# Shared keys as seven block products per pair of heads, the key gain in the norm, and the second adaLN's chunks at other places

## The chip, the cores and the metric

The kernel runs on one core of a Trainium2 chip. Its engines are TensorE (PE in the profile; PEld is its weight load), VectorE (DVE), ScalarE (ACT), GpSimd (POOL) and SyncE (SP), which issues most DMAs. The metric is the device time of one execution in microseconds. Times below are medians of runs, and where the profile is meant, those of one profiled execution.

## The reference, cut to what matters

One step of a two-layer encoder for 512 prompt tokens and 8 x 16 sample tokens (640 together, D = 2048, 16 heads of 128). Layer 0 is a recurrent layer, layer 1 an attention layer with keys and values that come from layer 0's output `x`:

```python
def ada_mod(c, w, b):
    m = jax.nn.silu(c) @ w + b
    shift, scale, gate = jnp.split(m, 3, axis=-1)
...
def shared_kv(x, g_kv, w_kv):
    k, v = jnp.split(rms_norm(x, g_kv) @ w_kv, 2, axis=-1)
...
def run_group(...):
    for l in range(DEPTH):
        shift, scale, gate = ada_mod(c, w_ada[l], b_ada[l])
        hn = rms_norm(x, g_pre[l]) * (1.0 + scale) + shift
        if l < N_A:
            out, hT, cb = recurrent_mixer(hn, ...)
        else:
            k_new, v_new = shared_kv(x, g_kv, w_kv)
            ...
            out = stick_breaking_mixer(hn, k_all, v_all, w_in_b[j], w_out_b[j])
        x = x + gate * rms_norm(out, g_post[l])
```

All is float32. `w_kv` is 2048 x 4096: keys for 16 heads, then values.

## The kernel before

Products in float32 accuracy are made of three in `fp32r`: each operand is split into a high part (ACT copies it, L87) and a low part (DVE subtracts, L88), and `mm3` (L101 to L103) adds high x high, high x low and low x high in PSUM. Weights pass through this split on the way: DMA into `wr`, `hilo` into `wh` and `wl`, three buffers each.

The stages after the recurrent layer, in order:

- *First output product* (`out_product`, tiles `acc`): the lower half of the rows of `w_out_a`, four chunks of 512 columns, all five token tiles; 16 K tiles in steps of two. At the end of each step of chunks 1 to 3 it advances a generator `fill` once.
- *Second output product*: the upper half, eight chunks (three token tiles x four columns, then two x four).
- *The norm* (`mid`): for each token tile t, residual, row norm, then for each of four column blocks n a scaled tile `nt`, four PE transposes into PSUM (`pst`, two banks), ACT's copy `nh` and DVE's rest `nl`. These, as `hT`, are the moving or stationary operand of all later products. POOL computes the powers of the row norms (`ss`, `sr`, L290) and issues the stores of `x1d`.
- *Shared keys and values* (`shared_kv`): `values(0)`, then `keys(h)` for 16 heads, then `values(1)` to `values(3)` (all tiles `acck`). A column of values is 16 K tiles x 5 token tiles x 3 products of 128x512; a head of keys is 16 K tiles x 2 halves of 320 tokens x 3 products of 128x320. The gain `g_kv` goes into the weights: for v within the split (L1029, L1030), for k by a POOL product over the raw weights (L1037). In `values(3)` `query_norm` turns `hT` in place into the attention layer's input, from the sum of `nh` and `nl`.

adaLN's vectors for layer 1 (and the gate of layer 0) are 16 chunks of 512 columns of `w_ada`. A chunk is four groups; a group (`ada`) loads two raw tiles `wa` (512 KB each), splits each into three bf16 parts (two ACT casts L185, two DVE subtractions L186), and runs 12 matmuls `psa` (L198) of 32 columns at four column places. Groups come from the `fill` generator: layer 0's gate in the first output product, the other 12 chunks (`ada_rest`) in the keys and in `values(1)` to `values(3)`.

The recurrent layer's input product already forms pairs of output blocks by a seven-product scheme (`pair_product`, `pair_weights`, `seven`): for a pair of 128-column blocks and 14 of the 16 K tiles, seven block products stand for eight; the two remaining K tiles are plain. Sums of weight quarters are made by DMAs that add (POOL's queue).

The order on each engine is set when the program is built, by a scheduler that works with estimated durations; on the chip every engine runs its own list strictly in that order, and a wait holds up all that stands behind it.

Of the kernel before, what the change touches and what calls it, by code (L numbers as in the profile page):

```python
# [19 lines left out]
P = 128  # L20
D = 2048
# [27 lines left out]
class Trunk:  # L49
# [32 lines left out]
    def hilo(self, raw, width):  # L82
# [4 lines left out]
        nc.scalar.activation(hi[:, :n], raw, AF.Copy)  # L87
        nc.vector.tensor_tensor(lo[:, :n], raw, hi[:, :n].bitcast(F32), ALU.subtract)  # L88
# [3 lines left out]
    def wraw(self, src, width):  # L92
        n = src.shape[1] * width
        raw = self.wp.tile([P, self.WW], F32, tag="wr", name="wr", bufs=self.RB)
        v = raw[:, :n].rearrange("p (a n) -> p a n", n=width)
        self.nc.sync.dma_start(v, src)
        return v
# [80 lines left out]
    def ada_split(self, src):  # L178

        nc = self.nc  # L180
        raw = self.adap.tile([P, 2, 512], F32, tag="wa", name="wa", bufs=self.abufs[0])
        nc.sync.dma_start(raw, src)
        parts = [self.adap.tile([P, 2, 512], BF16, tag=f"wa{i}", name=f"wa{i}", bufs=self.abufs[1]) for i in range(3)]
# [5 lines left out]
    def ada(self, w):  # L189
# [3 lines left out]
        ps = self.bank("psa")  # L193
        for g in range(4):
            ws = [self.ada_split(w[:, k : k + 2, :]) for k in (4 * g, 4 * g + 2)]
            for i in range(3):
                for j in range(4):
                    nc.tensor.matmul(ps[32 * j : 32 * j + 32, :], self.c3[:, 4 * g + j, :], ws[j // 2][i][:, j % 2, :],  # L198
                                     start=g + i == 0, stop=g == 3 and i == 2)
# [5 lines left out]
    def ada_cols(self, w, dst):  # L205

        for m in self.ada(w):
# [47 lines left out]
    def ada_gate(self, l, c):  # L255

        nc, I = self.nc, self.I
        for m in self.ada(I["w_ada1"][12 * l + c]):
# [14 lines left out]
    def ada_gates(self, l):  # L273
        for c in range(4):
            yield from self.ada_gate(l, c)

    def ada_rest(self):

        for part, dst in ((0, self.sh1), (1, self.gs1)):
            for c in range(4):  # L280
                dsts = [self.ada_dst(1, part, k, dst) for k in range(4 * c, 4 * c + 4)]
                yield from self.ada_cols(self.I["w_ada1"][4 + 4 * part + c], dsts)
        yield from self.ada_gates(1)
# [62 lines left out]
    def start(self, rp):  # L346
# [19 lines left out]
        for k in range(KD):  # L366
# [55 lines left out]
            elif k < 2 * NP:  # L422
                self.combine(rp, slot, even, tmp)
# [10 lines left out]
    def combine(self, rp, slot, even, odd):  # L434
# [3 lines left out]
        t = [rp.tile([P, HALF], F32, tag=f"s{i}", name=f"s{i}", bufs=1) for i in range(4)]  # L438
# [1120 lines left out]
```

## Time and profile before

| | us |
|---|---|
| median of 3 runs | 2882.94 (2881.82 to 2884.23) |
| profiled execution | 2886.43 |
| its span | 2884.3 |
| granted TensorE clock, mean | 0.996 |
| DMA | 546.33 MB, mean 189 GB/s |

The span reaches from the first instruction to the end of the last; the 2.1 us beyond it are the launch. Shares are of the span. A matmul's duration in the profile is a modelled latency; matmuls overlap, so what one costs is the distance from its start to the next one's. "PE busy" counts these overlapped records.

### The profile page before, as it was taken

Reading aid. Unit: us, or ns where it says so; the run is one execution under the profiler, and the core shown is the slowest. Engines: PE = TensorE matmul, PEld = TensorE weight load, DVE = VectorE, ACT = ScalarE, POOL = GpSimd, SP = SyncE. Lnnn points to the kernel's source line nnn. Section 1 sums busy time; section 2 is a strip of 40 time slices with the busy share of each in tenths; the row PEclk is TensorE's granted clock in tenths of the full one; section 3 lists DMA queues with packets and bytes.
Section 4 is the critical chain, followed back from the end, with each engine's and each line's share of the span. In section 5 each row is a group of like instructions: output and inputs, shape, how many; then the busy total and the mean of one; then the engine's idle time right before and its main releaser. Section 6 shows DMA issues by size and latency. Waiting matters only on the chain.

```text
span 2884.3 us, 48196 instructions
## 1 busy us (share of the span) xinstructions
PE 2826.2 (98%) x18784; PEld 2514.8 (87%) x18784; DVE 1965.5 (68%) x2865; ACT 1605.6 (56%) x2464; POOL 415.3 (14%) x604
## 2 busy tenths in 40 slices
PE   6999999999999999999999999999999999998998
PEld 5799999999999987788778999778989889996787
DVE  7678767777777767543678777767766677666235
ACT  5476556655665566443566666753555555555223
POOL 0012211221122100001114221001000001101000
PEclk9999999999999999999999999999999999999999
DMA  9966766676667565654757666654556656567637
GB/s 328 331 146 156 165 160 156 157 165 160 154 158 165 121 243 184 186 181 131 251 188 239 212 215 208 214 173 145 175 177 195 197 184 194 172 209 273 174 110 226
DMA packets 249363, 546.33 MB, mean 189 GB/s; under 512 B 23000, under 2 KB 107096, under 8 KB 247984
## 3 DMA queue, kind: packets, MB, share of 16 engines
q1 hardware_dynamic: 221216, 446.92, 48.5%
q0 software_dynamic: 27920, 96.34, 15.7%
q8 instruction: 147, 2.41, 0.3%
q14 instruction: 80, 0.66, 0.1%
HBM read 501.15 MB, written 42.02 MB: 188 GB/s over the span
## 4 chain that ended last, share of the span: by engine, by line
PE 86%; DVE 3%; DMA 2%; ACT 1%; issue 1%; POOL 0%; SPq 0%; DVEq 0%; POOLq 0%; ACTq 0%
PE acc L101 6%; PE acc L103 6%; PE acc L102 6%; PE psh L101 5%; PE acck L101 5%; PE psh L103 5%; PE psh L102 5%; PE acck L102 5%; PE acck L103 5%; PE pa L101 3%; PE pa L103 3%; PE pa L102 3%; PE pc L103 2%; PE pc L101 2%; PE pc L102 2%; PE psa L198 2%
## 5 line engine op out<-in xcount | busy, mean ns | idle before, releaser
L88 DVE TENSOR_TENSOR wl<-wr,wh 128x1024 fp32r<-128x1024 f32 x216 | 269.7, 1251 | 306.0 <-ACT wh L87 305.6
L87 ACT ACTIVATE wh<-wr 128x1024 fp32r<-128x1024 f32 x216 | 228.1, 1057 | 408.2 <-PE acc L103 257.2
L101 PE MATMUL acc<-wh,yh 128*128 128x512 f32 x960 | 376.8, 393 | 3.1 <-ACT wh L87 3.0
L102 PE MATMUL acc<-wl,yh 128*128 128x512 f32 x960 | 375.3, 391 | 3.5 <-DVE wl L88 3.5
L103 PE MATMUL acc<-wh,yl 128*128 128x512 f32 x960 | 373.9, 390 | 1.3 <-DVE yl L837 1.3
L101 PE MATMUL psh<-nh,wh 128*128 128x320 f32 x1024 | 324.1, 317 | 0.0
L186 DVE TENSOR_TENSOR wa<-wa,wa 128x1024 bf16<-128x1024 f32 (+1 forms) x256 | 306.4, 1233 | 22.0 <-ACT wa L185 20.0
L103 PE MATMUL psh<-nh,wl 128*128 128x320 f32 x1024 | 319.0, 312 | 0.0
L102 PE MATMUL psh<-nl,wh 128*128 128x320 f32 x1024 | 317.6, 310 | 0.0
L185 ACT ACTIVATE wa<-wa 128x1024 bf16<-128x1024 f32 x256 | 263.1, 1052 | 61.6 <-DVE wa L186 42.7
L101 PEld LDWEIGHTS acc<-wh,yh 128*128 128x128 f32 x960 | 180.2, 188 | 50.6 <-issue 8.5
L102 PEld LDWEIGHTS acc<-wl,yh 128*128 128x128 f32 x960 | 180.6, 188 | 42.9 <-DVE wl L88 6.2
L103 PEld LDWEIGHTS acc<-wh,yl 128*128 128x128 f32 x960 | 180.6, 188 | 39.2 <-DVE yl L837 1.7
L101 PEld LDWEIGHTS psh<-nh,wh 128*128 128x128 f32 x1024 | 192.4, 188 | 19.3 <-DVE ql L1183 12.6
L103 PE MATMUL pa<-xs,wl 128*128 128x320 f32 x630 | 194.9, 309 | 0.5 <-DVE wl L88 0.5
L102 PE MATMUL pa<-xs,wh 128*128 128x320 f32 x630 | 194.8, 309 | 0.0
L101 PE MATMUL pa<-xs,wh 128*128 128x320 f32 x630 | 194.8, 309 | 0.0
L103 PEld LDWEIGHTS psh<-nh,wl 128*128 128x128 f32 x1024 | 192.5, 188 | 0.5 <-DVE wl L88 0.2
L102 PEld LDWEIGHTS psh<-nl,wh 128*128 128x128 f32 x1024 | 192.4, 188 | 0.1
L101 PE MATMUL acck<-nh,wh 128*128 128x320 f32 x512 | 161.6, 316 | 0.0
L103 PE MATMUL acck<-nh,wl 128*128 128x320 f32 x512 | 158.3, 309 | 0.0
L102 PE MATMUL acck<-nl,wh 128*128 128x320 f32 x512 | 158.2, 309 | 0.0
(357 smaller groups left out, 7213.6 us busy)
## 6 DMA issues: line engine op xcount, KB each, us to landing
wa<-w_ada_dram SPq DMA_DIRECT2D x192, 512.0 KB, 4.6
wr<-w_out_a_dram SPq DMA_DIRECT2D x96, 512.0 KB, 4.0
sum<-w_in_a_dram POOLq DMA_DIRECT2D x90, 448.0 KB, 5.6
wr<-w_in_b_dram SPq DMA_DIRECT2D x64, 512.0 KB, 5.5
ck<-cache_k_dram SPq DMA_DIRECT2D x64, 512.0 KB, 6.8
cv<-cache_v_dram SPq DMA_DIRECT2D x64, 512.0 KB, 5.4
wr<-w_out_b_dram SPq DMA_DIRECT2D x56, 512.0 KB, 3.8
raw<-w_in_a_dram SPq DMA_DIRECT2D x60, 448.0 KB, 4.2
```

Source lines behind the costliest of these rows:

```text
L87: nc.scalar.activation(hi[:, :n], raw, AF.Copy)
L88: nc.vector.tensor_tensor(lo[:, :n], raw, hi[:, :n].bitcast(F32), ALU.subtract)
L101: mm(out, sh, mh, start=start, stop=False, **kw)
L102: mm(out, sh, ml, start=False, stop=False, **kw)
L103: return mm(out, sl, mh, start=False, stop=stop, **kw)
L185: nc.scalar.activation(parts[i], raw, AF.Copy)
L186: nc.vector.tensor_tensor(parts[2] if i else raw, raw, parts[i], ALU.subtract)
L198: nc.tensor.matmul(ps[32 * j : 32 * j + 32, :], self.c3[:, 4 * g + j, :], ws[j // 2][i][:, j % 2, :], start=g + i == 0, stop=g == 3 and i ...
```

## The change

The keys are computed in pairs of heads with the seven-product scheme, as in the recurrent layer: K tiles 0 to 13 in seven block products, tiles 14 and 15 plain. They come after `values(1)`; beside `values(1)`'s steps DVE and ACT build the four sums of halves of `hT` (tiles `ks`). `g_kv` is applied once, in the norm, so that `hT` holds the gained rows; the rows without it are stored to DRAM (`nd`) and loaded again by `query_norm`. The adaLN chunks move: shift 0 to 3 join layer 0's gate in the first output product (rate 1, 2, 1 per step), scale 0 to 3 go beside the second one (every second step), and the gate of layer 1 goes beside `values(2)` and `values(3)`. Three chunks (the last shift, the last two gates) are "whole": no bf16 split, one fp32 matmul each in place of three bf16 ones, with the summed vector `c1`. Raw weights use four single tags in rotation in place of one tag with four buffers.

```diff
-    def ada(self, w):
+    def ada(self, w, whole):
...
         for g in range(4):
-            ws = [self.ada_split(w[:, k : k + 2, :]) for k in (4 * g, 4 * g + 2)]
-            for i in range(3):
+            if whole:
+                ws = [[self.adap.tile([P, 2, 512], F32, tag=tag, name="wa", bufs=bufs)] for _ in range(2)]
+                for i, (x,) in enumerate(ws):
+                    nc.sync.dma_start(x, w[:, 4 * g + 2 * i : 4 * g + 2 * i + 2, :])
+            else:
+                ws = [self.ada_split(w[:, k : k + 2, :]) for k in (4 * g, 4 * g + 2)]
+            n = len(ws[0])
+            for i in range(n):
                 for j in range(4):
-                    nc.tensor.matmul(ps[32 * j : 32 * j + 32, :], self.c3[:, 4 * g + j, :], ws[j // 2][i][:, j % 2, :],
-                                     start=g + i == 0, stop=g == 3 and i == 2)
+                    nc.tensor.matmul(ps[32 * j : 32 * j + 32, :], (self.c1 if whole else self.c3)[:, 4 * g + j, :], ws[j // 2][i][:, j % 2, :],
+                                     start=g + i == 0, stop=g == 3 and i == n - 1)
...
                 if c > 0:
-                    next(fill, 0)
+                    for _ in range(rate[k // 2 % len(rate)]):
+                        next(fill, 0)
...
-            self.abufs = self.AB
+            self.atags = [("wa", 3)] + [(f"wa{i}", 4) for i in range(3)]
             with self.pool("ada") as self.adap:
-                rest = self.ada_gates(0)
+                rest = chain(*(self.ada_gate(0, c) for c in range(4)), *(self.ada_shift(0, c) for c in range(3)), self.ada_shift(0, 3, True))
...
+                self.adap, self.atags = bp, (("xx", 4), ("nt", 3), ("nq", 2), ("ns", 2))
+                rest = chain(*(self.ada_shift(1, c) for c in range(4)))
                 chunks = [(x, n) for x in ((0, 1, 2), (3, 4)) for n in range(4)]
-                for _ in self.out_product([self.yd[D:, :]], w[:, :, KD:, :], chunks, add):
+                for _ in self.out_product([self.yd[D:, :]], w[:, :, KD:, :], chunks, add, rest, (0, 1)):
...
-                nc.scalar.activation(hh[:, :, ts], pv, AF.Copy)
-                nc.vector.tensor_tensor(hl[:, :, ts], pv, hh[:, :, ts].bitcast(F32), ALU.subtract)
+                nq, ng = (bp.tile([P, 4, P], F32, tag=tag, name=tag, bufs=2) for tag in ("nq", "ns"))
+                nc.vector.tensor_tensor(ng, pv, self.gkv[:, 4 * n : 4 * n + 4].unsqueeze(2).broadcast_to([P, 4, P]), ALU.mult)
+                nc.scalar.activation(nq, pv, AF.Copy)
+                nc.gpsimd.dma_start(self.nd[512 * n : 512 * n + 512, ts].rearrange("(j p) t -> p j t", p=P), nq)
+                nc.scalar.activation(hh[:, :, ts], ng, AF.Copy)
+                nc.vector.tensor_tensor(hl[:, :, ts], ng, hh[:, :, ts].bitcast(F32), ALU.subtract)
...
         values(0)
-        for h in range(NHEAD):
-            keys(h)
-        for n in range(1, 4):
-            values(n)
+        with self.pool("sums") as sp:
...
+            def step(k):
+                if k < 2 * NP:
+                    slot = sp.tile([P, 2, 4 * HALF], F32R, tag="ks", name="ks", bufs=NP)
+                    t = [bp.tile([P, 512], F32, tag="kve", name="kt", bufs=6)[:, :HALF] for _ in range(4)]
+                    self.combine(t, slot, value(k), value(k + 1), (1, 2, 3, 0))
...
+            values(1, step=step)
...
+            for q in range(NHEAD // 2):
...
+                self.pair_product(evac)
+        with self.pool("queries") as self.qp, self.pool("ada") as self.adap:
+            self.atags = [("wa", 4)] + [(f"wa{i}", 4) for i in range(3)]
+            fill = chain(*(self.ada_gate(1, c, c > 1) for c in range(4)))
+            first, self.ready = self.ready, []
+            values(2, first, lambda k: [next(fill, 0) for _ in range(1 + (k % 4 == 0))])
+            values(3, (), lambda k: next(fill, 0))
...
-        tmp = self.more.tile([P, T], F32, tag="mod", name="mod1", bufs=2)
-        nc.vector.tensor_tensor(tmp, mh.bitcast(F32), ml.bitcast(F32), ALU.add)
+        tmp = self.qp.tile([P, T], F32, tag="mod", name="mod1", bufs=4)
+        nc.sync.dma_start(tmp, self.nd[P * k : P * k + P, :])
```

What the built programs show at three places follows. The first is PE, early in the groups of the first output product (`acc` its products, `c3` the vector as weights, `psa` the group's matmuls on the split parts `wa`). Before:

```order
L103 MATMUL acc_11686<-wh_11689,yl_11341 128x512
L198 LDWEIGHTS c3_121
L198 MATMUL psa_11723<-wa0_11726,c3_121 32x512
L198 LDWEIGHTS c3_121
L198 MATMUL psa_11723<-wa0_11726,c3_121 32x512
L198 LDWEIGHTS c3_121
L198 MATMUL psa_11723<-wa0_11735,c3_121 32x512
```

and in the fourth adaLN chunk of the changed program:

```order
L107 MATMUL acc_12340<-wl_12522,yh_11356 128x512
L210 LDWEIGHTS c3_122
L210 MATMUL psa_12458<-wa_12500,c3_122 32x512
L210 LDWEIGHTS c3_122
L210 MATMUL psa_12458<-wa_12500,c3_122 32x512
L108 MATMUL acc_12340<-wh_12521,yl_11357 128x512
L106 MATMUL acc_12341<-wh_12521,yh_11356 128x512
L210 LDWEIGHTS c3_122
L210 MATMUL psa_12458<-wa_12492,c3_122 32x512
L210 LDWEIGHTS c3_122
L210 MATMUL psa_12458<-wa_12492,c3_122 32x512
L107 MATMUL acc_12341<-wl_12522,yh_11356 128x512
```

Before, the 12 matmuls of each of the 64 groups stand together; now many groups are taken apart into runs of two or four, with products between them, 120 runs in all.

The second is ACT in the norm (`jk`, `jk1` squares for the row norms, `nt` the scaled tile). Before:

```order
L1008 ACTIVATE nh_14630<-pst1_14677 128x4x128
L885 ACTIVATE jk_14626,ss4_13123<-oacc4_11324 128x512
L1008 ACTIVATE nh_14632<-pst1_14686 128x4x128
L1002 ACTIVATE nt_14740<-oacc1_11321,sr1_13125 128x512
L1008 ACTIVATE nh_14634<-pst1_14695 128x4x128
```

and now:

```order
L1039 ACTIVATE nq_15647<-pst1_15642 128x512
L1041 ACTIVATE nh_15603<-ns_15648 128x4x128
L1039 ACTIVATE nq_15661<-pst1_15656 128x512
L1030 ACTIVATE nt_15721<-oacc1_11322,sr1_13570 128x512
L1041 ACTIVATE nh_15605<-ns_15662 128x4x128
L1030 ACTIVATE nt_15749<-oacc1_11322,sr1_13570 128x512
L900 ACTIVATE jk1_15873,sr3_13572<-oacc3_11324 128x512
L1039 ACTIVATE nq_15675<-pst1_15670 128x512
L1041 ACTIVATE nh_15607<-ns_15676 128x4x128
```

Each transposed tile takes two copies now, and the one to `nq`, which has two buffers, stands ahead of later `nt` and `nh`.

The third is POOL at the same place (`gm` the gate rows, `mhalf` the exponent of the row norm). Before:

```order
L290 TENSOR_TENSOR ss_13122<-ss_13122,mhalf 128x1
L993 DMA x1d<-oacc_11323 128x2048
L290 TENSOR_TENSOR sr_13127<-sr_13127,mhalf 128x1
L290 TENSOR_TENSOR ss_13123<-ss_13123,mhalf 128x1
L993 DMA x1d<-oacc_11324 128x2048
L290 TENSOR_TENSOR sr_13128<-sr_13128,mhalf 128x1
```

and now:

```order
L295 TENSOR_TENSOR ss_13567<-ss_13567,mhalf 128x1
L1040 DMA nd<-nq 128x4x128 x5
L1021 DMA x1d<-oacc_11324 128x2048
L1040 DMA nd<-nq 128x4x128 x4
L295 TENSOR_TENSOR sr_13572<-sr_13572,mhalf 128x1
L295 TENSOR_TENSOR ss_13568<-ss_13568,mhalf 128x1
L1040 DMA nd<-nq 128x4x128 x4
L1021 DMA x1d<-oacc_11325 128x2048
L1040 DMA nd<-nq 128x4x128 x3
L295 TENSOR_TENSOR sr_13573<-sr_13573,mhalf 128x1
```

The 20 stores of the rows without the gain stand between the powers of the row norms and the two stores of `x1d`.

236 lines of the change are left out of this document (125 added, 111 removed).

## The prediction

> **What bounds the kernel now.** I read the page's shares first, then the chain, then a table of busy time by stage, then the order of time at single places.
>
> ```profile
> span 2884.3 us, 48196 instructions
> PE 2826.2 (98%) x18784; PEld 2514.8 (87%) x18784; DVE 1965.5 (68%) x2865; ACT 1605.6 (56%) x2464; POOL 415.3 (14%) x604
> PE   6999999999999999999999999999999999998998
> PE 86%; DVE 3%; DMA 2%; ACT 1%; issue 1%; POOL 0%; SPq 0%; DVEq 0%; POOLq 0%; ACTq 0%
> ```
>
> TensorE (PE) is busy for 98% and carries 86% of the chain. The part that the change touches lies between 1018 and 1990 us. In the table of windows the columns are the stretch, its length, busy time and instructions of PE, PEld, DVE, ACT and POOL, the granted clock, the DMA share and GB/s. The rows are the first output product, the second one, the norm with v's first column, the keys, and v's columns 2 to 4.
>
> ```profile
> 1018.00:1257.10 239.10, 237.77 (x1162) 183.10 (x1161) 145.36 (x146) 132.30 (x153) 15.36 (x28) 1.00 0.63 200
> 1257.10:1477.40 220.30, 218.75 (x962) 179.93 (x962) 115.36 (x135) 98.59 (x143) 28.44 (x25) 1.00 0.59 186
> 1477.40:1544.80 67.40, 65.70 (x321) 52.44 (x320) 58.08 (x88) 51.15 (x89) 13.17 (x12) 1.00 0.66 231
> 1544.80:1806.20 261.40, 261.40 (x1978) 239.28 (x1977) 199.65 (x188) 174.55 (x200) 73.11 (x47) 1.00 0.66 212
> 1806.20:1989.90 183.70, 183.70 (x933) 139.41 (x930) 140.71 (x187) 109.04 (x139) 14.27 (x27) 1.00 0.52 167
> ```
>
> PE is busy from edge to edge at clock 1.00. So here time is what PE's own row of instructions costs, plus every wait that is added; PE's order is fixed, and a wait in it is made good nowhere. VectorE (DVE) is at 86% in the norm's row: the second engine that can bind.
>
> **The products that go.** A 128x320 product's price is the distance between starts:
>
> ```profile
> 1561.14 0.31 PE L103 MATMUL acck<-nh,wl 128*128 128x320 f32 x1
> ...
> 1565.98 0.31 PE L103 MATMUL acck<-nh,wl 128*128 128x320 f32 x1
> ```
>
> These starts are 33 instructions apart: 4.84 us / 33 = 0.147 us. The keys take 16 heads x 16 K tiles x 2 halves x 3 = 1536 products; after the change each of 8 pairs takes 7 x 7 + 4 x 2 = 57 block products of three, 1368. That is 168 x 0.147 = **-24.6 us**, all on the path.
>
> **The adaLN groups that move.** A group (psa) is 12 matmuls of 32 columns, four of which run beside each other. Around one:
>
> ```profile
> 1088.33 0.39 PE L101 MATMUL acc<-wh,yh 128*128 128x512 f32 x1
> 1088.55 0.39 PE L102 MATMUL acc<-wl,yh 128*128 128x512 f32 x1
> 1088.78 0.39 PE L103 MATMUL acc<-wh,yl 128*128 128x512 f32 x1
> 1089.10 0.83 PE L198 MATMUL psa<-wa,c 128*32 128x512 bf16 x12
> 1089.86 0.50 PE L101 MATMUL acc<-wh,yh 128*128 128x512 f32 x1
> 1090.19 0.39 PE L102 MATMUL acc<-wl,yh 128*128 128x512 f32 x1
> ```
>
> Products follow at 0.227 us, but 1.41 us lie from the last one ahead (1088.78) to the second one behind (1090.19): the run costs 1.41 - 2 x 0.227 = 0.955. Three slots of 512 columns are 3 x 0.227 = 0.68; the other 0.27 us is paid once a run, for going from full-width to 32-column matmuls and back (0.09 ahead of the run, 0.10 behind it, the rest inside). Another run shows the same ends, on fp32 tiles:
>
> ```profile
> 2075.21 0.31 PE L103 MATMUL psh<-nh,wl 128*128 128x320 f32 x1
> 2075.45 1.07 PE L1290 MATMUL zc<-ck,qs 128*32 128x512 f32 x8
> ...
> 2077.36 1.07 PE L1290 MATMUL zc<-ck,qs 128*32 128x512 f32 x8
> 2078.36 0.42 PE L101 MATMUL psh<-nh,wh 128*128 128x320 f32 x1
> 2078.61 0.31 PE L102 MATMUL psh<-nl,wh 128*128 128x320 f32 x1
> ```
>
> Ahead 0.24 instead of 0.147, behind 0.25; four fp32 matmuls of 32 columns (8 records) fill 1.00 us. That is the price of the three chunks that the change computes whole, in fp32.
>
> Before, all 64 groups are unbroken runs of 12. In the changed order they are 120 runs: 48 of 2, 34 of 4, 8 of 6, 17 of 12, 13 others; 14 of the 120 are fp32. The bf16 ones hold 185 slots in 106 runs, the fp32 ones 15 slots. Before: 192 x 0.227 + 64 x 0.27 = 60.9 us. After: 185 x 0.227 + 106 x 0.27 + 15 x 1.00 + 14 x 0.19 = 88.3 us. So the moved groups cost **+27.4 us**, 14 us of it in 56 more switches. What has no row is a run of 2 between full-width matmuls; its bounds are 0.23 (no switch) and 0.50 (a whole one), and I take 0.50, because runs of 8 and of 12 pay the same ends.
>
> The order of PE alone is thus -24.6 + 27.4 = +2.8 us. The gain is spent before anything waits.
>
> **The norm.** For each of 20 tiles the transposed rows (pst) were read by ACT (nh) and DVE (nl). Now DVE first multiplies them by g_kv (ns), ACT copies them out (nq) for a store through POOL's queue, and nh and nl are made of ns. These rows are of the norm's stretch; the first two are of the table of windows, the third tells when the transposes ran:
>
> ```profile
> 1473.50:1510.50 37.00, 35.30 (x187) 27.16 (x186) 34.37 (x67) 30.80 (x62) 4.77 (x6) 1.00 0.48 165
> 1477.40:1508.90 31.50, 29.80 (x163) 22.71 (x162) 29.77 (x58) 27.18 (x57) 4.67 (x6) 1.00 0.48 163
> L1005 PE MATMUL pst<-ident,nt x80: 269/273/330, 1477.4 to 1508.5; 128*128 128x128 f32 x80
> L1009 DVE TENSOR_TENSOR nl<-pst,nh 128x512 fp32r<-128x512 f32 x20 | 13.4, 685 | 0.4 <-ACT nh L1008 0.2
> L1030 DVE SCALAR_TENSOR_TENSOR wl<-wr,vec,wh 128x512 fp32r<-128x512 f32 x14 | 10.3, 745 | 0.0
> L1008 ACT ACTIVATE nh<-pst 128x512 fp32r<-128x512 f32 x20 | 11.5, 590 | 1.4 <-PE pst L1005 1.2
> ```
>
> DVE works 34.4 of 37.0 us here, 29.8 of the 31.5 us between first and last transpose. It gains 20 x 0.685 = 13.7 (L1009's row, which also reads PSUM) and loses about 2, since v's weights no longer carry g_kv (14 halves of 0.745 become 7 splits of 1.22). PE cannot pass: a transpose needs one of two banks that DVE and ACT free. So DVE alone adds 13.7 - 2 - (31.5 - 29.8) = **+10 us**.
>
> The second limit is nq, which has two buffers: the copy for tile n+2 waits until the store of tile n has landed. No row shows such a store with 512 B pieces; the nearest are v's (256 KB) and k's (320 KB) on that queue, and around one of v's:
>
> ```profile
> out_v_dram<-kve POOLq DMA_DIRECT2D x20, 256.0 KB, 3.4
> out_kT_dram<-ke POOLq DMA_DIRECT2D x16, 320.0 KB, 4.2
> x1d<-oacc POOLq DMA_DIRECT2D x5, 1024.0 KB, 8.3
> 1979.20 0.60 ACT L1054 ACTIVATE kve<-acck 128x512 f32<-128x512 f32 x1 [0.98 <-PE acck L103]
> 1980.09 0.56 POOL L1055 DMA_DIRECT2D out_v_dram<-kve  x1 [34.07 <-ACT kve L1054]
> ```
>
> A round is copy 0.59, hand-over 0.29 (1979.80 to 1980.09), landing 3.4 to 4.2: 4.3 to 5.1 us for two tiles, so that the 18th copy ends 8 rounds and about 1 us in, at 35 to 42 us, and the last transpose follows it; twice a 1 MB store of x1d is queued ahead on POOL. Before it came 31.1 us in (1477.4 to 1508.5). That is +4 to +11, about the same as DVE. Both chains go through strictly ordered ACT and DVE, so they hold each other up: I take **+13**, bounds +5 (half of v's 8.5 us of splits slip behind the last transpose) and +25 (every store 1.3 us later).
>
> [...]
>
> **Other waits.** *First output product*: 32 groups instead of 16 now lie in three chunks of its four. These rows price a split, two ACT and two DVE instructions on one raw tile, and its load:
>
> ```profile
> L186 DVE TENSOR_TENSOR wa<-wa,wa 128x1024 bf16<-128x1024 f32 (+1 forms) x256 | 306.4, 1233 | 22.0 <-ACT wa L185 20.0
> L185 ACT ACTIVATE wa<-wa 128x1024 bf16<-128x1024 f32 x256 | 263.1, 1052 | 61.6 <-DVE wa L186 42.7
> wa<-w_ada_dram SPq DMA_DIRECT2D x192, 512.0 KB, 4.6
> ```
>
> A raw buffer is held 4.6 + 2 x 1.05 + 2 x 1.23 = 9.2 us; with three of them a group of two splits comes every 6.1 us at best. PE needs one every (720 x 0.227 + 45) / 32 = 6.5 us (45 is the share of these eight chunks in the 88.3). So it just keeps up: 0 to 10, I take 4. *Second output product*: its fifth chunk, of two token tiles, takes four groups whose split parts have only two or three buffers, where loads already are late:
>
> ```profile
> 1420.70 1.06 ACT L87 ACTIVATE wh<-wr 128x1024 fp32r<-128x1024 f32 x1 [2.50 <-DMA wr<-w_out_a_dram]
> ```
>
> 0 to 8, I take 4. *Keys and last columns*: the sums beside v's second column are priced by those of the first layer,
>
> ```profile
> L448 DVE TENSOR_TENSOR xs<-s,xs 128x320 fp32r<-128x320 f32 x28 | 12.5, 483 | 1.0 <-ACT xs L447 1.0
> ```
>
> eight such and two of double width, 5.7 us for a pair of K tiles, with a split of 1.2 just PE's 30 x 0.227 = 6.8 us; seven of the eight steps carry them, so they are covered, and without that cover each us of lag is one of PE. The first groups beside v's third column can load only when the sums' memory is free: 0 to 3, I take 1. What left the keys, 32 POOL products and the split of 48 groups, freed engines that did not bind.
>
> **Sum**: -24.6 + 27.4 + 13 + 4 + 4 + 1 = +25 us. The profiled execution took 2886.4 us for its 2884.3 us span, 3.5 us above the median of 2882.94; from that median I predict **2908 us**.
>
> **Rivals.**
> - *Switches and short runs are nearly free.* If a run of 2 fills a hole in which PE would have waited for its split, the 14 us of added switches and the waits of 4 + 4 fall away, and with the norm at its lower bound the sum is -24.6 + 27.4 - 14 + 5 + 1 = -5: about 2878. It decides at about 0.1 us a switch. For it: the scheduler breaks runs where it expects a late split. Against: DVE had only 145 of 239 us of work in the first output product, and a hole that is filled at full price is still paid. This is the case that is not slower, 16%; of it half is faster by more than 0.2%.
> - *The store of the norm binds.* If the pieces of 512 B make issue or landing 1.3 to 2 us longer, a round takes 6 to 7 us and the last transpose comes 50 to 57 us in: +19 to +26 instead of +13, so 2914 to 2921. For it: x1d's 1 MB stands ahead on the queue. Against: nothing shows that smaller pieces cost more there. 20%.
> - *The keys don't reach 0.147 us.* Each pair's sums of weights are made by adding DMAs, as in the recurrent layer; should one be late in each pair by 1.5 us, that is 8 x 1.5 = +12: 2920. Against: the recurrent layer (up to 1010 us: slices 3 to 14 of the page's row of PE above, in tenths) runs the same plan with PE at 9 tenths or more. 9%.
> - Forecast as summed: 55%, within 2896 to 2916.
>
> **How the numbers follow.** About 0.2%, 6 us, is what a measurement of this kernel can tell from no change. The first rival's half below 2877 gives faster 0.09; its other half, with the low edge of the forecast, same 0.11; all the rest slower 0.80. The range takes the first rival's centre and both others: 2879 to 2932.
>
> **What would show it.** Right: the keys' block products fill about 201 us at steps of 0.147; the first output product grows from 239 to about 275, the second from 220 to about 247; a psa run of 2 takes PE 0.5 us; PE waits on transposes for 10 us or more in the norm, released by nq's or ns's readers. Wrong: PE's steps around short runs of psa are those of a plain product; the norm keeps its 31 us; or the keys take 215 us or more.

## The result, and the profile after

The changed kernel takes 2924.11 us (2923.28 to 2930.67, 4 runs), the kernel before 2883.59 us: 1.0144 times as long, 95% interval [1.0126, 1.0162]. The forecast was +25 us, it became +41. That lies inside the range on record (2879 to 2932), but above the 2896 to 2916 that the sum had for itself and above its rivals' 2921. The page of the changed kernel, span, busy time of the engines, TensorE's row of slices and the chain of work that ended last:

```profile
span 2922.4 us, 47866 instructions
PE 2846.4 (97%) x18568; PEld 2496.6 (85%) x18568; DVE 1967.2 (67%) x2926; ACT 1589.7 (54%) x2464; POOL 402.9 (14%) x640
PE   7999999999999999999998999999999999999998
PE 82%; DVE 3%; issue 3%; DMA 3%; ACT 2%; POOL 0%; SPq 0%; DVEq 0%; POOLq 0%; ACTq 0%
```

PE holds 82% of the chain instead of 86%: waits have come into it. Where they stand, the table of windows shows, columns as in the prediction. The rows are the first output product, the second one, the norm with v's first column, v's second column, the keys, and v's last two columns:

```profile
1014.00:1290.20 276.20, 270.71 (x1350) 190.77 (x1348) 205.10 (x211) 181.36 (x207) 10.96 (x19) 0.99 0.66 214
1290.20:1549.20 259.00, 252.37 (x1206) 190.85 (x1205) 191.30 (x215) 158.83 (x208) 36.82 (x34) 0.98 0.75 244
1549.20:1635.70 86.50, 72.10 (x321) 57.16 (x320) 57.93 (x88) 51.01 (x87) 21.46 (x29) 0.92 0.65 202
1635.70:1690.10 54.40, 54.40 (x242) 45.06 (x241) 41.04 (x76) 22.68 (x42) 5.06 (x8) 1.00 0.43 112
1690.10:1892.10 202.00, 202.00 (x1371) 200.70 (x1369) 82.73 (x103) 71.37 (x106) 44.20 (x63) 1.00 0.74 180
1892.10:2033.00 140.90, 138.90 (x650) 92.66 (x649) 86.15 (x118) 64.50 (x75) 11.78 (x22) 1.00 0.71 236
```

Two things are new beside the lengths: PE is idle for 28.5 us in these stretches (length less busy time; 4.6 before), and the granted clock is below 1.00 in three of them (0.99, 0.98, 0.92).

| stretch (us) | before | forecast | after |
|---|---|---|---|
| first output product | 239.1 | about 275 | 276.2 |
| second output product | 220.3 | about 247 | 259.0 |
| norm and v's first column | 67.4 | 80.4 (67.4 + 13) | 86.5 |
| keys (before: with half of the groups) | 261.4 | about 201 | 202.0 |
| from the first output product to the end of the values | 971.9 | 996.9 (971.9 + 25) | 1019.0 |

The last row is +47 us; 4 us come back ahead of it and 5 behind it, where the change touches little beside the raw weights' tags. The stretch ahead ends between 1014 and 1026 us in the profiles of this study, as the first adaLN's loads land sooner or later (PE waits 3.7 us for them in the changed kernel, 8.3 in e1_unbroken, 11.6 in e6_combined). So kernels are compared by their stretches as well as by their medians. This table gathers them from the traces (starts of the first product of each stretch):

| kernel | 1st output product | 2nd | norm, v's 1st column | v's last two columns | median us |
|---|---|---|---|---|---|
| after | 276.2 | 259.0 | 86.5 | 141.0 | 2924.1 |
| e1_unbroken | 266.3 | 252.0 | 86.6 | 136.4 | 2910.4 |
| e2_no_store | 274.7 | 253.8 | 77.1 | 140.8 | 2913.3 |
| e3_no_gkv | 275.8 | 256.2 | 81.3 | 140.5 | 2918.5 |
| e4_unbroken_held | 264.8 | 254.9 | 89.8 | 136.8 | 2911.5 |
| e5_moved_left_out | 257.8 | 224.5 | 87.6 | 114.5 | 2850.6 |
| e6_combined | 262.4 | 256.0 | 83.1 | 147.3 | 2921.9 |
| e7_combined_spread | 263.9 | 256.1 | 82.2 | 148.3 | 2921.7 |
| e8_store_on_act | 275.8 | 256.7 | 78.4 | 140.9 | 2918.9 |
| e9_all_whole | 261.6 | 244.3 | 86.6 | 137.0 | 2895.5 |
| e10_all_whole_store_act | 261.5 | 244.3 | 78.3 | 133.7 | 2889.0 |
| e11_pairs_of_groups | 259.2 | 239.8 | 78.3 | 131.0 | 2876.5 |
| e12_pairs_no_store | 259.1 | 240.4 | 75.9 | 130.1 | 2875.6 |

### The profile page after: what moved, and what is told of

It is laid out like the page before. It is cut to its first block, busy times and chain, and to the rows that moved or that the text cites. A ratio compares the mean times of both kernels' runs of the same rounds, so it can differ in the third digit from the quotient of the medians.

```text
span 2922.4 us, 47866 instructions
## 1 busy us (share of the span) xinstructions
PE 2846.4 (97%) x18568; PEld 2496.6 (85%) x18568; DVE 1967.2 (67%) x2926; ACT 1589.7 (54%) x2464; POOL 402.9 (14%) x640
## 4 chain that ended last, share of the span: by engine, by line
PE 82%; DVE 3%; issue 3%; DMA 3%; ACT 2%; POOL 0%; SPq 0%; DVEq 0%; POOLq 0%; ACTq 0%
PE acc L106 6%; PE acc L108 6%; PE acc L107 6%; PE psh L106 6%; PE psh L108 5%; PE psh L107 5%; PE pa L106 4%; PE pa L108 4%; PE pa L107 4%; PE pc L106 3%; PE pc L108 3%; PE pc L107 3%; PE acck L106 2%; PE acck L107 2%; PE acck L108 2%
## 5 line engine op out<-in xcount | busy, mean ns | idle before, releaser
L92 DVE TENSOR_TENSOR wl<-wr,wh 128x1024 fp32r<-128x1024 f32 x256 | 319.2, 1248 | 253.6 <-ACT wh L91 253.0
L91 ACT ACTIVATE wh<-wr 128x1024 fp32r<-128x1024 f32 x256 | 270.1, 1056 | 369.6 <-PE acc L108 176.1
L106 PE MATMUL acc<-wh,yh 128*128 128x512 f32 x960 | 383.3, 400 | 5.4 <-ACT wh L91 5.4
L191 DVE TENSOR_TENSOR wa<-wa 128x1024 bf16<-128x1024 f32 (+1 forms) x208 | 248.9, 1234 | 47.1 <-ACT wa L190 45.6
L190 ACT ACTIVATE wa<-wa 128x1024 bf16<-128x1024 f32 x208 | 210.2, 1049 | 82.5 <-DMA wa<-w_ada_dram 56.8
L91 ACT ACTIVATE wh<-sum 128x896 fp32r<-128x896 f32 x114 | 108.3, 950 | 172.9 <-PE pa L107 62.5
L92 DVE TENSOR_TENSOR wl<-sum,wh 128x896 fp32r<-128x896 f32 x114 | 123.9, 1087 | 55.1 <-ACT wh L91 41.2
L524 POOL DMA_DIRECT2D sum<-w_in_a_dram x90 | 79.8, 890 | 489.8 <-DVE wl L92 209.8
```

What stands on the lines that cost most here:

```text
L106: mm(out, sh, mh, start=start, stop=False, **kw)
L190: nc.scalar.activation(parts[i], raw, AF.Copy)
L191: nc.vector.tensor_tensor(parts[2] if i else raw, raw, parts[i], ALU.subtract)
L524: self.nc.gpsimd.dma_start(self.big[tag], self.quarter(w, i), accum_op=ALU.add)
```

## The experiments

All edits are to the changed kernel. First the groups' order and the norm, each alone.

### e1_unbroken

```diff
-            for i in range(n):
-                for j in range(4):
+            for i in reversed(range(n)):
+                for j in (2, 3, 0, 1):
...
-                                     start=g + i == 0, stop=g == 3 and i == n - 1)
+                                     start=g == 0 and i == n - 1, stop=g == 3 and i == 0)
```

> Edit: each group of the adaLN products issues its matmuls in reverse order of the split parts, so that its first matmul already needs the part that is made last; in TensorE's order the groups then are 63 runs (50 of 12, 12 of 4, one of 24) in place of 120. Everything else of the changed kernel (2924 us) stays. Theory of the prediction (each switch between full-width and 32-column matmuls costs 0.27 us of PE, whatever stands inside): 57 switches fewer x 0.27 = -15 us, 2909 us; the first output product falls from 276 to about 267, a whole run of 12 takes 0.96. Rival (a short run fills time in which PE would have waited for the last split anyway): PE's waits ahead of the runs grow by what the switches save; less than 5 us come back, 2919 us or more.

Measured: 2910.4 us, 1.0092 [1.0077, 1.0107] of before; the first output product -9.9, the second -7.0, the last two columns -4.6. What a broken run costs stands in TensorE's timeline of the changed kernel (start, duration):

```profile
1161.84 0.40 PE L106 MATMUL acc<-wh,yh 128*128 128x512 f32 x1
1162.16 0.39 PE L210 MATMUL psa<-wa,c 128*32 128x512 bf16 x2
1162.49 0.50 PE L107 MATMUL acc<-wl,yh 128*128 128x512 f32 x1
1162.82 0.40 PE L108 MATMUL acc<-wh,yl 128*128 128x512 f32 x1
```

From 1161.84 to 1162.82 are 0.98 us; less two steps of 0.227, a run of two matmuls costs 0.53, where 0.50 was forecast. The first output product of e1_unbroken shows the other side:

```profile
1116.13 0.39 PE L108 MATMUL acc<-wh,yl 128*128 128x512 f32 x1
1116.45 0.83 PE L210 MATMUL psa<-wa,c 128*32 128x512 bf16 x12
1117.21 0.50 PE L106 MATMUL acc<-wh,yh 128*128 128x512 f32 x1
1119.37 0.83 PE L210 MATMUL psa<-wa,c 128*32 128x512 bf16 x12 [1.66 <-DVE wa L191]
1120.13 0.50 PE L107 MATMUL acc<-wl,yh 128*128 128x512 f32 x1
```

A whole run is cheap, but PE now waits ahead of many of them for DVE's last split (9.3 us in this output product, against 4.2 ahead of groups before the edit). Its row of the table of windows in e1_unbroken:

```profile
1020.20:1286.50 266.30, 255.55 (x1347) 189.58 (x1345) 203.34 (x211) 179.84 (x206) 10.96 (x19) 1.00 0.67 221
```

Over the three stretches PE's busy time falls by 28.6 us and its idle time grows by 7.1, so they are 21.5 us shorter. The median shows 13.7 of it, because in the profile the stretch ahead ends 6.2 us later and the one behind is 1.6 us longer. Both theories hold in part: the switches come back, and some of them had filled waits. That the median met the switch theory's 15 us is luck: the theory counts 0.27 us for each run that goes, but a broken run also costs slots that are filled in part (0.53 us for a run of two as for one of four), and the waits and the stretch ahead took the surplus away again.

### e2_no_store, e3_no_gkv, e8_store_on_act

e2_no_store takes out the copy nq and its store and rebuilds the queries' input:

```diff
-                nc.scalar.activation(nq, pv, AF.Copy)
-                nc.gpsimd.dma_start(self.nd[512 * n : 512 * n + 512, ts].rearrange("(j p) t -> p j t", p=P), nq)
...
+            nc.vector.reciprocal(rg, self.gkv)
+            nc.vector.tensor_tensor(self.gs1, self.gs1, rg.unsqueeze(2).broadcast_to([P, KD, NG]), ALU.mult)
...
-        nc.sync.dma_start(tmp, self.nd[P * k : P * k + P, :])
+        nc.vector.tensor_tensor(tmp, mh.bitcast(F32), ml.bitcast(F32), ALU.add)
```

> Edit: nq and its store to DRAM are taken out of the norm; the queries' norm adds nh and nl again, as the kernel before did, with g_kv divided out of its scale (a reciprocal and one multiplication once). The product with g_kv (ns) stays. From first to last transpose the changed kernel takes 48.5 us, the kernel before 31.1. Theory DVE (the prediction's first limit): without nq, ACT and the store's landing out of the way, DVE alone is left, 31.1 + 10 = about 41 us, so -7 us, 2917 us. Theory store binds: the transposes come back to 31 to 36 us, -13 to -17 us and the halved clock behind the waits goes with them, 2907 to 2911 us. Theory that the store was never waited for: 47 to 49 us, 2922 us or more.

Measured: 2913.3 us, 1.0103 [1.0088, 1.0118]; transposes over 42.7 us, norm and v's first column 77.1. The row of that stretch:

```profile
1545.40:1622.50 77.10, 67.92 (x321) 54.27 (x320) 57.27 (x88) 42.23 (x66) 6.91 (x9) 0.98 0.50 160
```

The second output product, which this edit leaves alone, is 5.2 us shorter as well, so the median alone would not tell what the store costs.

e3_no_gkv:

```diff
-                nc.vector.tensor_tensor(ng, pv, self.gkv[:, 4 * n : 4 * n + 4].unsqueeze(2).broadcast_to([P, 4, P]), ALU.mult)
...
-                nc.scalar.activation(hh[:, :, ts], ng, AF.Copy)
-                nc.vector.tensor_tensor(hl[:, :, ts], ng, hh[:, :, ts].bitcast(F32), ALU.subtract)
+                nc.scalar.activation(hh[:, :, ts], pv, AF.Copy)
+                nc.vector.tensor_tensor(hl[:, :, ts], pv, hh[:, :, ts].bitcast(F32), ALU.subtract)
```

> Edit: the product with g_kv (ns) is left out, so keys and values are computed without g_kv; nq and its store stay, nh and nl read the transposed rows themselves. Theory DVE: the transposes fall from 48.5 us to about 38, -10 us, 2914 us. Theory store binds: nq's two buffers still wait for the store's landing, 45 us or more, at most -3 us, 2921 us or more. If both fall by much, the two are one chain in which ACT and DVE, each strictly in order, wait for each other.

Measured: 2918.5 us, 1.0123 [1.0107, 1.014]; transposes 47.4 us, the stretch 81.3. The transposes stay as long as the theory of the store has it; the stretch is 5.2 us shorter, mostly because 91 of v's products stand ahead of the last transpose, where the changed kernel has 73. Three rows of the table of waits (engine, what, for whom: total us, times, longest) of its norm and first column:

```profile
DVE nl L1041 <- ACT nh L1040: 13.2, 11, 2.8
ACT nq L1038 <- DMA nd<-nq: 11.2, 9, 3.0
PE acck L106 <- ACT nh L1040: 7.1, 3, 3.1
```

nq waits for the store, nh stands behind it on ACT, and both PE and DVE wait for nh. Three rows of the same table of the changed kernel:

```profile
PE pst L1033 <- ACT nq L1039: 10.1, 8, 2.6
ACT nh L1041 <- DVE ns L1038: 5.8, 4, 1.9
ACT nq L1039 <- DMA nd<-nq: 3.9, 4, 2.8
```

Here PE waits for ACT's copy, ACT for the store and for DVE's product: the two chains hold each other up. e2_no_store gives DVE's share alone, 77.1 - 67.4 = +9.7 us, where +10 was forecast. The store brings another 9.4 (86.5 - 77.1).

e8_store_on_act asks what of the store it is:

```diff
-                nc.gpsimd.dma_start(self.nd[512 * n : 512 * n + 512, ts].rearrange("(j p) t -> p j t", p=P), nq)
+                nc.scalar.dma_start(self.nd[512 * n : 512 * n + 512, ts].rearrange("(j p) t -> p j t", p=P), nq)
```

> Edit: the changed kernel, with nq's store issued by ACT's own queue instead of POOL's; nothing else. In e3_no_gkv nq waited 8 times for such a store, 8.2 us in all, with nh and nt behind it on ACT. Theory (the round of a buffer is copy, hand-over, landing, and POOL's queue with x1d's stores ahead adds to it): ACT's queue takes the hand-over away, the transposes fall from 48.5 us to 44 or less, 2920 us or less. Rival (landing and ACT's own order decide): 47 us or more, no change of the time.

Measured: 2918.9 us, 1.0116 [1.0101, 1.0132]. The transposes still end after 48.3 us, as the rival has it, but PE gets more of v's products done between them: 108 stand ahead of the last transpose in place of 73, and the 35 more at 0.227 are 8.0 us. The stretch is 78.4 us, -8.1. Neither theory had looked at that; the span of the transposes was the wrong measure. The store's rows (KB each, median us to landing) before and after this edit:

```profile
nd<-nq POOLq DMA_DIRECT2D x20, 256.0 KB, 2.9
```

```profile
nd<-nq ACTq DMA_DIRECT2D x20, 256.0 KB, 2.5
```

Copy to issue takes 0.29 to 0.70 us over POOL and 0.03 on ACT; a buffer's shortest round is 3.71 us before and 3.26 after. But ACT waits for stores here no less (6.1 us, 3 times, against 3.9 us, 4 times). By the count of products the 8 us are the order in which the scheduler, with its new estimate, put v's products among the transposes; what the shorter round would have given in the old order was not separated.

### e4_unbroken_held

In the changed kernel's second output product, PE's longest wait there, in its timeline and in ACT's:

```profile
1319.20 0.39 PE L108 MATMUL acc<-wh,yl 128*128 128x512 f32 x1
1322.56 0.79 PE L106 MATMUL acc<-wh,yh 128*128 128x512 f32 x1 [2.98 <-ACT wh L91]
1324.01 0.80 PE L107 MATMUL acc<-wl,yh 128*128 128x512 f32 x1 [0.66 <-DVE wl L92]
1324.60 0.63 PE L108 MATMUL acc<-wh,yl 128*128 128x512 f32 x1
1325.03 0.63 PE L106 MATMUL acc<-wh,yh 128*128 128x512 f32 x1
...
1329.57 0.39 PE L108 MATMUL acc<-wh,yl 128*128 128x512 f32 x1
```

```profile
1320.51 1.06 ACT L190 ACTIVATE wa<-wa 128x1024 bf16<-128x1024 f32 x1 [12.06 <-DMA wa<-w_ada_dram]
```

ACT stood 12 us at an adaLN group's split whose load was late; the output weights' split was next in its order. The steps behind the wait are 0.43 us instead of 0.227: the granted clock is 0.50 from 1322.55 to 1329.38. The 15 steps from 1319.20 to 1329.57 took 10.4 us where 15 x 0.227 = 3.4 are needed, so 3.6 us of waiting, with the steps behind them, cost 7.0.

```diff
                     for _ in range(rate[k // 2 % len(rate)]):
-                        next(fill, 0)
+                        if hold:
+                            with self.tc.issue_after(self.last_wr), self.tc.issue_after(self.last_wh):
+                                next(fill, 0)
+                        else:
+                            next(fill, 0)
```

(`hold` is set for the second output product; `last_wr` and `last_wh` are the last load and the last high part of the output weights. e1_unbroken's edit is in as well.)

> Edit: as e1_unbroken, and in the second output product the loads and the first splits of each adaLN group are ordered behind the load and the split of the output weights of their own step. In the changed kernel PE waited there 3.4 us at 1319 us, ACT being held for 12 us by a group's split whose load had not landed, and the granted clock was 0.50 for the next 6 us. Theory (ACT's strict order turns the late load into PE's wait, and the wait lowers the clock): the second output product is 6 to 7 us shorter than in e1_unbroken, clock 1.00 throughout, 2902 us. Rival (the DMA engines are full there, the output weights come late whatever the order): PE waits as long at the same step, 2907 us or more.

Measured: 2911.5 us, 1.0096 [1.0081, 1.0111], the second output product 254.9 against e1_unbroken's 252.0. Nothing was gained: e1_unbroken's longest wait near there is 0.8 us already, and with the groups held, PE waits 0.9 to 1.2 us ahead of four of them for their last split. The halved clock did not go either: the mean granted clock of the execution is 0.992, as in e1_unbroken (0.98 there in this output product). So how long this wait is varies with the loads from kernel to kernel; e2, e3 and e8, which keep the order, have 254 to 257 us in this stretch.

### e5_moved_left_out

```diff
+        if self.skip:
+            m = self.more.tile([P, 512], F32, tag="mod", name="msb", bufs=2)
+            nc.gpsimd.memset(m, 0.0)
+            yield m
+            return
```

(`skip` is set for the second adaLN and for layer 1's gates.)

> Edit: the twelve adaLN chunks that the change moved (48 groups: second adaLN's shift and scale and the last gates) are left out, with their loads, splits and matmuls; zeros stand in for their result, so queries and gates of the second layer are computed from zeros. The first four chunks stay beside the first output product. Theory (the groups themselves, with the waits for their splits, make the three stages long): the first output product falls from 276 to about 240 us, the second from 259 to about 226, v's last two columns from 141 to about 112; in all about -98, 2826 us. So the 48 groups cost about 98 us where they are now. Rival (the second output product is long because the gate maps and larger row loads fill the DMA engines there, not because of groups): it stays at 240 us or more, 2842 us or more.

Measured: 2850.6 us, 0.988 [0.9865, 0.9895]; -73.5 us instead of -98. The second output product (224.5) and the last two columns (114.5) are as the theory had them, the first (257.8) is not: the 16 groups that stay stand so close there that they cost 23.5 us in place of 15.3, with waits inside three runs of 24. That is 8 of its 19 us over the kernel before. Another 7 is the clock: its mean there is 0.97, with 0.91 from 1110 to 1130 us and 0.74 from 1190 to 1210, and (0.09 + 0.26) x 20 = 7.0 us. The second of these is beside the psc products of the chunks left out, which now stand close together; and 4 are these psc products themselves (32). So leaving out 48 groups brings 74 us, less than they cost, because the edit adds some of its own; at 0.96, before's price of a run, they would be 46.

### e6_combined and e7_combined_spread

On top of e1_unbroken's and e2_no_store's edits:

```diff
-                for _ in self.out_product([self.yd[D:, :]], w[:, :, KD:, :], chunks, add, rest, (0, 1)):
+                for _ in self.out_product([self.yd[D:, :]], w[:, :, KD:, :], chunks, add, rest, (1, 0, 1)):
...
-                nc.vector.tensor_tensor(hl[:, :, ts], ng, hh[:, :, ts].bitcast(F32), ALU.subtract)
+                (nc.gpsimd if n % 2 else nc.vector).tensor_tensor(hl[:, :, ts], ng, hh[:, :, ts].bitcast(F32), ALU.subtract)
...
-            fill = chain(*(self.ada_gate(1, c, c > 1) for c in range(4)))
+            fill = chain(*(self.ada_gate(1, c) for c in range(4)))
```

> Edit: e1_unbroken and e2_no_store together, and three more: of the second output product's steps two in three carry a group (instead of every second one), so that all 16 lie beside the chunks of three token tiles; the last two chunks of gates are split like the others, not whole; in the norm every second nl is made on POOL. Theory (waits for splits come where a step of PE is shorter than DVE's work for it): from 2910 us, -11 for the store, -10 in the second output product (252 to about 242), -5 in the norm (42.7 to about 38), -2 for the gates: about 2882 us. Rival (DVE has 13.5 us of work in 14.2 us of the three-tile steps, so the waits only move there): the second output product stays at 249 us or more and the kernel at 2890 or more.

Measured: 2921.9 us, 1.0126 [1.0108, 1.0143], no better than the changed kernel. The rival held: the second output product is 256.0 us. The norm's stretch is 83.1, 6 us more than without POOL's nl; and the last two columns grew by 11 us over e1_unbroken (147.3). There the last two chunks are now split, and the queries' rows are added on DVE. e2_no_store adds them too, with the chunks whole, and has 140.8 against the changed kernel's 141.0; so the splits are the likelier cause, though no run has them alone. The trace agrees: PE waits there 8.6 us for DVE's splits of the groups and 4.2 us for its low parts of v's weights.

> Edit: e6_combined, and the first output product takes one group in each of its 32 steps, from its first chunk on, instead of four groups in three steps from the second chunk on. Theory (DVE then has 6.2 us of work in a step of 7.8): its waits ahead of groups, 9.3 us in e1_unbroken, fall to 1 or 2, the stage from 266 to about 257 us, the kernel about 9 us below e6_combined, 2873 us. Rival (the first chunk already carries the splits of the 16 rows of its other operand, 7.6 us of DVE work in 7.8): the waits move into the first chunk, the stage stays at 263 us or more.

```diff
-                if c > 0:
+                if c >= since:
...
-                for _ in self.out_product([self.yd[0:D, :]], w[:, :, 0:KD, :], chunks, keep, rest, (1, 2, 1), urgent=True):
+                for _ in self.out_product([self.yd[0:D, :]], w[:, :, 0:KD, :], chunks, keep, rest, (1,), urgent=True, since=0):
```

Measured: 2921.7 us, 1.0125 [1.0106, 1.0144]; the first output product 263.9, so the rival again. Moving split groups about does not help.

### e9_all_whole, e10_all_whole_store_act

All groups whole, with e1_unbroken's order; e10 adds the edit of e8_store_on_act. Beside the first output product and v's last columns the memory of the split parts goes to loaded tiles, eight in place of three or four; beside the second output product the four stay.

```diff
+        whole = True
         tag, bufs = self.atags[0]
...
-            self.atags = [("wa", 3)] + [(f"wa{i}", 4) for i in range(3)]
+            self.atags = [("wa", 8)]
```

> Edit: all 16 adaLN chunks are computed whole, in fp32 from the loaded tile, none is split; the groups are unbroken as in e1_unbroken, and the memory of the split parts goes to loaded tiles (eight in place of three or four). A whole group costs PE 1.19 us where an unbroken split one without a wait costs 0.96. Theory (the waits are for the splits, and the halved clock follows the waits): 64 groups at 1.2 are 77 us against 85 of e1_unbroken's, and the late splits of the output weights behind them on ACT and DVE go too: first output product 266 to about 261 us, second 252 to about 245, last two columns 136 to about 131, together -17 on e1_unbroken's 2910, 2893 us. Rival (the waits stay, because loads and not splits are late): the dearer groups add 64 x 0.24 = 15 us, 2920 us or more.

Measured: 2895.5 us, 1.0038 [1.0025, 1.0052], as the theory said (2893), though each group is dearer on PE. The second output product's row of the table of windows in e1_unbroken and in this kernel:

```profile
1286.50:1538.40 251.90, 246.41 (x1212) 190.66 (x1209) 191.60 (x215) 159.20 (x208) 36.40 (x34) 0.98 0.78 251
```

```profile
1279.80:1524.10 244.30, 242.54 (x1133) 186.13 (x1130) 115.63 (x150) 97.22 (x142) 35.89 (x34) 1.00 0.75 250
```

At the same GB/s, DVE falls from 191.6 to 115.6 us, PE's idle time from 5.5 to 1.8, and the clock is 1.00 again. The splits, not the loads, were late; in the first output product, where the loads got more buffers too, the two are not separated. Only the last two columns missed (137.0 instead of 131): a 2.7 us wait for the first load is part of it, the rest was not separated.

> Edit: e9_all_whole, and nq's store issued by ACT's queue as in e8_store_on_act. There the stretch from the first transpose to the keys fell from 140.9 to 132.7 us. Theory (the two act in different stages and add up): 8 us below e9_all_whole, about 2885 us if that comes to 2893. Rival (they share a limit, ACT's order): less than 4 us.

Measured: 2889.0 us, 1.0016 [1.0007, 1.0025], 6.5 below e9_all_whole (8 in the theory; the norm's stretch is 8.3 us shorter): the parts add up.

### e11_pairs_of_groups, e12_pairs_no_store

On top of e10_all_whole_store_act; e12 has e2_no_store's edit in place of e8's.

```diff
-                for _ in self.out_product([self.yd[0:D, :]], w[:, :, 0:KD, :], chunks, keep, rest, (1, 2, 1), urgent=True):
+                for _ in self.out_product([self.yd[0:D, :]], w[:, :, 0:KD, :], chunks, keep, rest, (0, 2, 2, 0, 2, 2, 0, 3), urgent=True):
...
-                for _ in self.out_product([self.yd[D:, :]], w[:, :, KD:, :], chunks, add, rest, (0, 1)):
+                for _ in self.out_product([self.yd[D:, :]], w[:, :, KD:, :], chunks, add, rest, (0, 0, 0, 2)):
...
-            values(2, first, lambda k: [next(fill, 0) for _ in range(1 + (k % 4 == 0))])
-            values(3, (), lambda k: next(fill, 0))
+            values(2, first, lambda k: [next(fill, 0) for _ in range(3 * (k % 4 == 2))])
+            values(3, (), lambda k: [next(fill, 0) for _ in range(2 * (k % 4 == 2))])
```

> Edit: e10_all_whole_store_act with the whole groups issued two or three at a time, on fewer steps, so that two or more stand behind each other in TensorE's order: 33 runs in place of 54; beside v's third column they begin one step later. In e10 a run of one group takes 1.20 us, one of two 2.06. Theory (a switch is paid once a run): 21 runs fewer x 0.34 = -7 us, and the 2 us wait for the first load beside v's third column goes: 2880 to 2882 us, below the kernel before (2885). Rival (two groups at a time need their loads sooner, and PE waits for them): 2887 us or more.

Measured: 2876.5 us, 0.9972 [0.9962, 0.9983]: 0.3% faster than the kernel before, and below the 2880 to 2882 of the theory: the stretches account for 9.5 of the 12.5 us against e10, where 9 were expected. The same six stretches in its table of windows, v's first two columns in one row:

```profile
1019.20:1278.40 259.20, 257.86 (x1251) 189.29 (x1249) 77.44 (x101) 74.83 (x98) 10.96 (x19) 1.00 0.67 238
1278.40:1518.20 239.80, 239.12 (x1132) 187.71 (x1129) 113.00 (x149) 96.34 (x139) 34.88 (x34) 1.00 0.76 252
1518.20:1651.00 132.80, 123.67 (x562) 98.67 (x561) 99.12 (x163) 74.13 (x127) 11.03 (x17) 0.99 0.61 178
1651.00:1852.90 201.90, 201.90 (x1370) 200.64 (x1369) 82.72 (x103) 71.21 (x107) 44.09 (x63) 1.00 0.74 180
1852.90:1983.80 130.90, 129.43 (x617) 93.27 (x616) 49.64 (x86) 33.60 (x43) 11.56 (x22) 1.00 0.71 252
```

PE's idle time outside the norm is down to 3.5 us, the clock at 1.00.

> Edit: e11_pairs_of_groups, with the store of the norm left away and rebuilt as in e2_no_store instead of issued by ACT. Theory (with the store on ACT's queue, what is left of the norm's lengthening is DVE's product with g_kv): the stretch from first transpose to keys stays at 131 to 133 us, the same time as e11 within 3 us. Rival (ACT's copies and issues still cost there): 4 us or more below e11.

Measured: 2875.6 us, 0.9971 [0.9963, 0.998]; the norm's stretch is 2.4 us shorter, the time the same as e11's. The theory holds nearly (130.2 us from first transpose to keys); e11 has no division by g_kv and is the one to keep.

## Why the prediction was right, and where it was short

- **The products that go** (-24.6): right. The keys take 202 us at steps of 0.147 in these kernels (203 in e5_moved_left_out); the rival of late weight sums falls.
- **The moved groups** (+27.4): the price of a switch was right (0.53 for a run of two, 0.96 for twelve, 1.19 for a whole group), and e1_unbroken got 21.5 us of its three stretches back with the switches. A run of two or four was taken at 0.50 and costs 0.53; on 82 such runs that is 2.5 us too little. So the rival "switches and short runs are nearly free" falls.
- **The norm** (+13): measured 86.5 - 67.4 = +19.1, the low end of the rival "the store binds" (+19 to +26). By the two tables of windows PE's idle time there grew by 12.7 us (1.7 to 14.4), which is what +13 stood for. The other 6.4 is busy time: the same 321 matmuls take 72.1 us in place of 65.7, at a granted clock of 0.92, and for that the sum had nothing. What the waits would have been at full clock no run shows. DVE's +10 came out at 9.7 (e2_no_store), 2.2 of it again longer busy time. The store adds 9.4 on top, where "both chains ... hold each other up: I take +13" left 3 for it: the transposes are 5.8 us longer, and 16 fewer of v's products stand ahead of the last one. The landings of that rival, 1.3 to 2 us later, are met by some stores alone, and that their small pieces make them late was not shown. The median lands in 2.9 us, less than the 3.4 to 4.2 assumed, but six of the 20 take 4.5 to 6.9; three of these were issued while a store of x1d was under way, and nq's longest wait (2.8 us) is for one of them.
- **Other waits** (4 + 4 + 1): PE's idle time grew by 4.2, 5.1 and 2.0 us in these stretches, 11.3 against 9; with the norm's it is 24 against 22, so as lengths the waits were nearly right. Yet against the forecast the first output product is 1 us over, the second 12, and v's last two columns 2 (996.9 less the other forecasts and 54.4 for the second column leaves 139 for them), 15 in all. Of the first two, 2.7 and 4.5 are psc products (24 and 40 at 0.112) that stood beside the keys and v's columns before; they cancel in the sum, though not in its stretches. If the forecasts of the first two left them out, the second is over by 7.5 and the last two columns by 9. What brings the waits e9_all_whole shows: the two output products fall by 4.7 and 7.7 us where nothing is split, with dearer matmuls.
- **The clock** (nothing): this is the step that failed. A wait was priced at its length, while in the changed kernel the granted clock is 0.50 behind several of them: for 3.4 us in the first output product, 10.2 in the second, 13.7 in the norm. Half of PE's busy time in these times at half clock is 1.7 + 4.8 + 6.2 = 12.7 us, more than half of what the sum was short.

One wait was mis-sized: beside v's third column 1 us was allowed for the first group, and PE waits 2.0 us for it, 1.82 of them here:

```profile
1894.31 0.39 PE L210 MATMUL psa<-wa,c 128*32 128x512 bf16 x2 [1.82 <-ACT wa L190]
```

The sum was thus short by 22 us between the first output product and the values (+47 against +25): 13 are the halved clock, 2 longer waits, 2.5 the short runs, and about 5 stay unassigned. The 9 us that came back on either side were not forecast and made the total look closer; that is luck.

## What to carry to other kernels

Where one engine is busy from edge to edge, work that is moved beside it is paid in full, plus every wait that its preparation brings: leaving out the preparation (fp32 at 1.19 us a group instead of three bf16 parts at 0.96) and issuing two groups behind each other won more than any other placement of split groups. A gain of 24 us in one stage can be spent twice by what had to leave that stage; price the new place of the moved work by the chain behind one unit of it, not by the share of busy time, and allow for more than a wait's length: at 1319 us in the changed kernel 3.6 us of waiting cost 7.0, with the granted clock at 0.50 behind them. Measure a stage to its end, not to the last instruction of one kind: e8's gain would not have been seen in its transposes.

## What the runs showed of the hardware

In the changed kernel, between 1005 and 2035 us, the granted clock is 0.50 in six stretches and 1.00 in all the rest; 128x512 products follow there at 0.427 us instead of 0.227. PE's waits ahead of them, or at their start, are in its timeline:

| clock 0.50 from | for (us) | PE's waits there (us), the last one's end |
|---|---|---|
| 1114.34 | 3.41 | 1.07 and 0.86, 1113.73 |
| 1322.55 | 6.83 | 2.98, 1322.56 |
| 1482.98 | 3.41 | 1.82 and 0.69, 1481.73 |
| 1561.49 | 3.41 | 1.31, 0.96 and 1.44, 1560.90 |
| 1568.31 | 3.41 | 2.56, 1568.43 |
| 1581.97 | 6.83 | 0.45, 0.41 and 2.51, 1583.08 |

The length of one wait does not tell it: the wait of 2.61 us that ends at 1552.90 has products at 0.23 to 0.24 us behind it, and so has one of 1.82 us that ends at 1894.31, at clock 1.00 both, while 1.07 and 0.86 us with 0.4 between them have clock 0.50 behind them. In the kernel before, whose longest wait in its part of that time is 1.29 us, the clock is 1.00 throughout. What decides between these cases was not shown.

Runs of two and of four matmuls of 32 columns cost the same 0.53 us (medians in the changed kernel), and two whole groups behind each other 2.06 (e11_pairs_of_groups) where two apart cost 2.40 (e10_all_whole_store_act).
